# Moving two small bursts of fp32 products in a scan: the reads beside the next block's masked products, the values' part beside the first corner product

## The chip, the cores and the metric

The kernel runs on one core of one Trainium2 chip. The metric is the device time of one execution in microseconds (us); the median of the runs before the change is 2252.5 us.

## The reference, cut to what matters

One inference step of a hybrid backbone with one layer, on 128 context tokens and 256 latent tokens (384 columns together), model width 2048. A large input projection feeds two branches. Branch A is a scan over time with 32 heads of size 64, once forward and once backward:

```
def step(S, inp):
    r_t, w_t, k_t, v_t, a_t, b_t = inp
    sa = einsum('dbhij,dbhj->dbhi', S, a_t)
    S = S * w_t[..., None, :] + sa[..., :, None] * b_t[..., None, :] + v_t[..., :, None] * k_t[..., None, :]
    y = einsum('dbhij,dbhj->dbhi', S, r_t)
    return S, y
y = ys[0] + ys[1]
mu = mean(y); var = mean((y - mu) ** 2)            # per head
y = ((y - mu) * rsqrt(var + GN_EPS)) * lnx_g + lnx_b
y = y + bonus
y_a = (y * silu(g_a)) @ w_out_a
```

Branch B is a short gated convolution. Both are gated, merged and projected again. The step by sa takes something out of the state ("removal") along a_t; S @ r_t is the "read".

## The kernel before, in words

**The projection stream.** Most of TensorE's work is one long stream of projections (`Stream`, L111). A unit of it is three matmuls (L81 to L83, a product in three parts of 128x128 weights by 384 columns). A pair of 128 output columns takes 32 units. The order of TensorE's work is written out by hand: `ds_.go(n)` emits n units, and between them the code emits the scan's small bursts of plain fp32 matmuls, whose generators yield how many units follow (`drive`, L931). An fp32 matmul that is not a transpose is two instructions in the profile, so 24 of them show as x48. The other engines' queues are ordered by a planner from its own costs and from the order in which the code emits, with `high_priority` for the scan.

**A block.** The scan works through 16 blocks of two heads (`for b in range(NB)`, L949), each cut into 6 chunks of 64 tokens a direction, 12 in all (index f). In a chunk the steps are solved together with a 64x64 triangular inverse, made from two 32x32 diagonal inverses and a corner.

- `prep_b` (L664) makes the operands pr and bk on VectorE, waits PB0 = 14 units, and emits the masked products: a burst of pA (L700) for one direction, masks on VectorE (L706) into the tile A, PB1 = 6 units, and the same for the other direction. It then writes the 32x32 diagonal blocks out through DRAM (L710), loads them as U (L716), inverts them on VectorE with 60 dependent operations (L721, L723), transposes them on ScalarE (UT, L727), and brings both back through DRAM into A (L734) and x11 (L735). POOL scales bk in between (L713).
- `prep_c` (L737) transposes the values into sav (pv, L755) and the keys into bt (pb, L764), a unit behind each. Then comes the values' part of the removals: pav (L770), 24 products of A's rows 64 to 127 with the values, four copies on ScalarE into sav (L774), and a clearing of A's used part on POOL (L777). It ends with sums for the bonus and a transpose of the state that is loaded (psi, L786).
- The driver goes on with the stream until the pair gv{b} is done, and then `prep_a` (L608) of the next block with its products; at least WINDOW = 80 units lie between the masked products and the scan.
- `scan` (L790) begins with the first corner product pH (L848 by way of L852), which needs A and x11, copies it into x11 (L854), starts the second chain (po, L810; the sum into sav on VectorE, L811), makes the second corner product pX (L867) and copies it into A (L869). Two chains then run through the chunks in bursts of two matmuls (po, pq, pu). At the end it reads within the chunks: py (L889), 24 products of A's second half with sav, added to the tile ytok on VectorE (L892). The states are transposed and written out (pso, L896).
- `norm` (L903) normalises ytok: VectorE, with one operation on ScalarE (L912) and one on POOL (L917). It is emitted behind the scan.
- `finish` (L920) of a block is emitted in the next one, just ahead of its masked products: three transposes (L924), then scale, bonus and gate (L926 to L928) and a write to ya_d (L929).

**What is shared.** The scan's PSUM results rotate through five banks (`bank`, L590). SP's queue issues nearly all DMAs in order: the weights' (L101, L104), the blocks' and the results'.

Of the kernel before, what the change touches and what calls it, by code (L numbers as in the profile page):

```python
# [12 lines left out]
ALU = mybir.AluOpType  # L13
AX = mybir.AxisListType

P = 128
# [4 lines left out]
NB = 16  # L21
C = 64
NCH = 6
# [33 lines left out]
def hybrid_step(ctx, tc, cst, x_prompt, x_sample, state_f, state_b, c, c_ctx, ada_w, ada_b, norm_g,  # L57
# [3 lines left out]
    V, S, G, TE = nc.vector, nc.scalar, nc.gpsimd, nc.tensor  # L61
# [120 lines left out]
    ds_ = Stream()  # L182
# [218 lines left out]
    r_, k_, v_, ga_ = {}, {}, {}, {}  # L401
# [188 lines left out]
    def bank(nm):  # L590
        return ps1.tile([P, 4, P], F32, tag="A", name=nm, bufs=5)
# [4 lines left out]
    def flat(a):  # L596
        return a.rearrange("p n t -> p (n t)")
# [66 lines left out]
    def prep_b(b, o):  # L664

        r, kk = r_[b], o["kk"]
        o["pr"], o["bk"] = [], []
        for d in range(2):
            ep, em, kd, bn = o["ep"][d], o["em"][d], o["kd"][d], o["bn"][d]
            pr = sp.tile([P, NCH, P], F32, tag=f"pr{d}", name=f"pr_{b}_{d}")  # L670
            bk = sp.tile([P, NCH, P], F32, tag=f"bk{d}", name=f"bk_{b}_{d}")
            V.tensor_tensor(bk[:, :, 0:C], c3(bn[:]), c3(em[:]), ALU.mult)
            V.tensor_tensor(bk[:, :, C:P], c3(kd[:]), c3(em[:]), ALU.mult)
            V.tensor_tensor(pr[:, :, 0:C], c3(kk[:, ::-1] if d else kk[:]), ep[:, :, 0:C], ALU.mult)
            r3 = c3(r[:])
            if d == 0:
                V.tensor_tensor(pr[:, :, C:P], r3, ep[:, :, 1:C + 1], ALU.mult)
            else:
                V.tensor_tensor(pr[:, :, C:P], r3[:, ::-1, :], ep[:, :, C:0:-1], ALU.mult)
            o["pr"].append(pr)  # L680
            o["bk"].append(bk)
        yield PB0

        def blocks(A, d, e):

            es = slice(32 * e, 32 * e + 32)
            return A[es, 0, NCH * d:NCH * d + NCH, :].rearrange("s n (h t) -> s (n h) t", h=2)[:, :, es]

        ui = dp.tile([2, 2, 12, 32, 32], F32, tag="ui", name=f"ui_{b}", bufs=2)
        uo = dp.tile([2, 2, 2, 12, 32, 32], F32, tag="uo", name=f"uo_{b}", bufs=2)  # L690

        A = sp.tile([P, 2, 2 * NCH, P], F32, tag="A", name=f"A_{b}")
        o["A"] = A
        for d in range(2):
            pr, bk = o["pr"][d], o["bk"][d]
            m0 = C_MB if d else C_MF
            pas = {(h, n0): bank(f"pA_{b}_{d}_{h}_{n0}") for n0 in (0, 4) for h in range(2)}
            for n in range(NCH):
                for h in range(2):
                    TE.matmul(pas[h, n // 4 * 4][:, n % 4, :], bk[hss[h], n, :], pr[hss[h], n, :],  # L700
                              start=True, stop=True)
            for n0, w in ((0, 4), (4, 2)):
                mk = cs[:, m0:m0 + P].rearrange("p (w t) -> p w t", t=C).unsqueeze(1).broadcast_to([P, w, 2, C])
                for h in range(2):
                    f0 = NCH * d + n0
                    V.tensor_tensor(A[:, :, f0:f0 + w, hss[h]].rearrange("p w n t -> p n w t"),  # L706
                                    pas[h, n0][:, 0:w, :].rearrange("p n (w t) -> p n w t", t=C), mk, ALU.mult)
            yield PB1
            for e in range(2):
                nc.sync.dma_start(ui[d, e].rearrange("i s t -> s i t"), blocks(A, d, e))  # L710

        for d in range(2):
            G.tensor_tensor(o["bk"][d][:], o["bk"][d][:], o["ep"][d][:, :, C:C + 1].broadcast_to([P, NCH, P]), ALU.mult)  # L713

        U = sp.tile([48, 32, 32], F32, tag="U", name=f"U_{b}")
        nc.sync.dma_start(U[:], ui[:].rearrange("d e i s t -> (d e i) s t"))  # L716
        ut = sp.tile([48, 256], F32, tag="ut", name=f"ut_{b}")
        for s in range(1, 31):
            w = 31 - s
            tv = ut[:, 0:s * w].rearrange("p (a b) -> p a b", b=w)  # L720
            V.tensor_tensor(tv, U[:, 0:s, s:s + 1].broadcast_to([48, s, w]),  # L721
                            U[:, s:s + 1, s + 1:].broadcast_to([48, s, w]), ALU.mult)
            V.tensor_tensor(U[:, 0:s, s + 1:], U[:, 0:s, s + 1:], tv, ALU.add)  # L723
        dg = U[:].rearrange("p a b -> p (a b)")[:, 0:1024:33]
        V.tensor_scalar(dg, dg, 1.0, None, ALU.add)
        UT = sp.tile([48, 32, 32], F32, tag="UT", name=f"UT_{b}")
        S.copy(UT[:], U[:].rearrange("p a b -> p b a"))  # L727
        nc.sync.dma_start(uo[0].rearrange("d e i s t -> (d e i) s t"), U[:])
        nc.sync.dma_start(uo[1].rearrange("d e i s t -> (d e i) s t"), UT[:])
        x11 = sp.tile([64, 24, 32], F32, tag="x11", name=f"x11_{b}")  # L730
        o["x11"] = x11
        for d in range(2):
            for e in range(2):
                nc.sync.dma_start(blocks(A, d, e), uo[0, d, e].rearrange("i s t -> s i t"))  # L734
            nc.sync.dma_start(x11[0:32, 12 * d:12 * d + 12, :], uo[1, d, 0].rearrange("i s t -> s i t"))  # L735

    def prep_c(b, o):  # L737

        r, v, A = r_[b], v_[b], o["A"]
        for d in range(2):  # L740
            for h in range(2):
                nc.sync.dma_start(s_in[d][hss[h], hss[h]], ctx_st[d][0, 0, 2 * b + h])
# [16 lines left out]
        for d in range(2):  # L759

            for n0, n1 in (((0, 4), (4, 5)), ((0, 3), (4, 6)))[d]:
# [2 lines left out]
                    TE.transpose(pb[:, n - n0, :], o["bk"][d][:, n, :], ident)  # L764
                S.copy(bt[:, NCH * d + n0:NCH * d + n1, :], pb[:, 0:n1 - n0, :])
                yield 1
        pvs = [bank(f"pav_{b}_{d}") for d in range(2)]
        for f in range(2 * NCH):
            for h in range(2):
                TE.matmul(flat(pvs[f // NCH][hss[h]])[:, C * (f % NCH):C * (f % NCH) + C], A[C:P, 0, f, hss[h]],  # L770
                          sav[C:P, f, hss[h]], start=True, stop=True)
        for d in range(2):
            for h in range(2):
                S.copy(sav[0:C, NCH * d:NCH * d + NCH, hss[h]],  # L774
                       flat(pvs[d][hss[h]])[:, 0:NCH * C].rearrange("p (n i) -> p n i", i=C))

        G.memset(A[C:P, 0, :, :], 0.0)  # L777
        yield 2
        ks = o["kd"]
        V.tensor_tensor(ks[0][:], ks[0][:], ks[1][:, ::-1], ALU.add)  # L780
        V.scalar_tensor_tensor(ks[0][:], ks[0][:], pcol(RK + b), r[:], ALU.mult, ALU.mult)
# [8 lines left out]
    def scan(b, o):  # L790
# [52 lines left out]
        def corner(nm, lhs, rhs):  # L843
# [5 lines left out]
                              start=True, stop=True)  # L849
            return [flat(pz[32 * j:32 * j + 32])[:, 0:192].rearrange("p (n t) -> p n t", t=32) for j in range(4)]  # L850

        pz = corner("pH", lambda f, h: A[0:32, 0, f, C * h + 32:C * h + C], lambda f, h: x11[0:32, 2 * f + h, :])  # L852
        for j in range(4):
            (S.copy, V.tensor_copy)[j % 2](x11[32:64, j::4, :], pz[j])  # L854
        yield H0
        lat = chain(1)
        next(lat)
# [22 lines left out]
                else:  # L880
                    yield CH0 if len(live) > 1 else CH1

        py = bank(f"py2_{b}")
        for q in range(3):
            for h in range(2):
                for d in range(2):
                    for e in range(2):
                        f = 2 * q + e if d == 0 else NCH + 5 - 2 * q - e
                        TE.matmul(py[hss[e], q, hss[h]], A[:, 1, f, hss[h]], sav[:, f, hss[h]],  # L889
                                  start=d == 0, stop=d == 1)  # L890
        yield 1
        V.tensor_tensor(ytok[:], ytok[:], py[:, 0:3, :], ALU.add)  # L892

        pt = bank(f"pso_{b}")
        for d in range(2):
            TE.transpose(pt[:, d, :], st[0][:, d, :], ident)  # L896
        for d in range(2):
# [2 lines left out]
                S.copy(nst[hss[h], :], pt[hss[h], d, hss[h]])  # L900
            nc.sync.dma_start(ctx_ns[d][0, 0, 2 * b:2 * b + 2].rearrange("h i j -> (h i) j"), nst[:])

    def norm(b, o):  # L903

        ytok = o["ytok"]
        y6 = ytok[:].rearrange("p q (h i) -> p (q h) i", i=C)
        mu = sp.tile([P, 6], F32, tag="mu", name=f"mu_{b}")
        V.tensor_reduce(mu[:], y6, AX.X, ALU.add)
        V.tensor_scalar(mu[:], mu[:], 1.0 / C, None, ALU.mult)
        V.tensor_tensor(y6, y6, mu[:].unsqueeze(2).broadcast_to([P, 6, C]), ALU.subtract)  # L910
        sq = tmp(f"ysq_{b}")
        S.activation(sq[:], flat(ytok[:]), AF.Square)  # L912
        var = sp.tile([P, 6], F32, tag="var", name=f"var_{b}")
        V.tensor_reduce(var[:], sq[:].rearrange("p (q i) -> p q i", i=C), AX.X, ALU.add)
        V.tensor_scalar(var[:], var[:], 1.0 / C, GN_EPS, ALU.mult, ALU.add)  # L915
        rs = sp.tile([P, 6], F32, tag="rs", name=f"rs_{b}")
        G.tensor_tensor(rs[:], var[:], nhalf[:], ALU.pow)  # L917
        V.tensor_tensor(y6, y6, rs[:].unsqueeze(2).broadcast_to([P, 6, C]), ALU.mult)
# [26 lines left out]
    cur = {}  # L945
# [3 lines left out]
    for b in range(NB):  # L949
# [5 lines left out]
        pb_gen = prep_b(b, cur)  # L955
        ds_.go(next(pb_gen))
        if prev is not None:
            finish(b - 1, prev)
        drive(pb_gen)
        n = drive(prep_c(b, cur))  # L960
        nxt = {}
        if b < NB - 1:
            while f"gv{b}" not in ds_.done:
# [10 lines left out]
                prep_k(b + 1, nxt)  # L974

        drive(scan(b, cur), 300, 3 if b < NB - 1 else None, keys)
        norm(b, cur)
        prev, cur = cur, nxt
    ds_.go(12)
    finish(NB - 1, prev)  # L980
    ctx_sc.close()

# [177 lines left out]
```

## Time and profile before

| | |
|---|---|
| median of 3 runs | 2252.5 us (2251.61 to 2254.43) |
| the profiled execution | 2250.97 us, its span 2249.2 us |
| granted TensorE clock of it | 0.996 |
| DVE, ACT, POOL busy | 68%, 47%, 5% of the span |
| chain that ended last | PE 84%, DVE 6%, DMA 6%, ACT 2% |

PE is TensorE's matmuls, PEld its weight loads, DVE VectorE, ACT ScalarE, POOL GpSimd, SP the engine that issues DMAs (SPq, its queue). A row of the timeline has the start (us from the span's start), the length, engine, line, operation, output tile <- input tiles, shapes, how many were merged, and in brackets the engine's idle time ahead of it and what ended that. The numbers ahead of a matmul's shape, as in 64\*64, are the rows and columns of TensorE that it uses. In a row of the windows view each engine has its busy time and count of instructions. Matmuls overlap in the records, so a burst's cost is read from start to start.

### The profile page before, as it was taken

Reading aid. Unit: us, or ns where it says so; the run is one execution under the profiler, and the core shown is the slowest. Engines: PE = TensorE matmul, PEld = TensorE weight load, DVE = VectorE, ACT = ScalarE, POOL = GpSimd, SP = SyncE. Lnnn points to the kernel's source line nnn. Section 1 sums busy time; section 2 is a strip of 40 time slices with the busy share of each in tenths; the row PEclk is TensorE's granted clock in tenths of the full one; section 3 lists DMA queues with packets and bytes.
Section 4 is the critical chain, followed back from the end, with each engine's and each line's share of the span. In section 5 each row is a group of like instructions: output and inputs, shape, how many; then the busy total and the mean of one; then the engine's idle time right before and its main releaser. Section 6 shows DMA issues by size and latency. Waiting matters only on the chain.

```text
span 2249.2 us, 40427 instructions
## 1 busy us (share of the span) xinstructions
PE 2191.4 (97%) x16084; PEld 2071.0 (92%) x16084; DVE 1522.2 (68%) x3096; ACT 1060.7 (47%) x1864; POOL 115.5 (5%) x115
## 2 busy tenths in 40 slices
PE   6999999999999999999999999999999999999998
PEld 3588999999999999999999999999999999889988
DVE  3249567787777778777878787777767774444454
ACT  4245445454545455455545454546455543333233
POOL 2000010101010100000010101010100000000000
PEclk9999999999999999999999999999999999999999
DMA  9963544444444445354434444344445455985633
GB/s 337 346 204 116 146 130 131 111 129 114 111 132 112 120 119 125 111 132 106 126 102 132 111 117 127 110 122 135 121 125 139 147 175 162 312 303 185 220 131 113
DMA packets 429644, 339.96 MB, mean 151 GB/s; under 512 B 84800, under 2 KB 411024, under 8 KB 428560
## 3 DMA queue, kind: packets, MB, share of 16 engines
q1 hardware_dynamic: 427968, 335.62, 51.0%
q8 instruction: 127, 2.08, 0.4%
q10 hardware_dynamic: 432, 1.57, 0.2%
q14 instruction: 61, 0.50, 0.1%
q0 software_dynamic: 1056, 0.19, 0.1%
HBM read 307.37 MB, written 29.36 MB: 150 GB/s over the span
## 4 chain that ended last, share of the span: by engine, by line
PE 84%; DVE 6%; DMA 6%; ACT 2%; issue 1%; SPq 1%; POOLq 0%; POOL 0%; DVEq 0%; ACTq 0%
PE d_rk L81 4%; PE d_rk L83 4%; PE d_rk L82 4%; DMA raw_adah<-in_ada_w_dram 4%; PE d_gv L81 4%; PE d_gv L83 4%; PE d_gv L82 4%; PE d_oa L81 2%; PE pA L700 2%; PE d_oa L83 2%; PE d_oa L82 2%; PE d_mb L81 2%; PE d_bc L81 2%; PE d_gb L81 2%; PE d_bg L81 2%; PE d_mb L83 2%
## 5 line engine op out<-in xcount | busy, mean ns | idle before, releaser
L81 PE MATMUL d_rk<-h_hi,whi_rk 128*128 128x384 f32 x480 | 164.4, 342 | 0.6 <-ACT lst L549 0.6
L721 DVE TENSOR_TENSOR ut<-U 48x30 f32<-48x30 f32 (+14 forms) x480 | 154.5, 322 | 15.3 <-DMA U<-ui 2.5
L723 DVE TENSOR_TENSOR U<-U,ut 48x30 f32<-48x30 f32 (+14 forms) x480 | 154.2, 321 | 11.2
L81 PE MATMUL d_gv<-h_hi,whi_gv 128*128 128x384 f32 x480 | 161.1, 336 | 0.0
L83 PE MATMUL d_gv<-h_hi,wlo_gv 128*128 128x384 f32 x480 | 161.0, 335 | 0.0
L82 PE MATMUL d_gv<-h_lo,whi_gv 128*128 128x384 f32 x480 | 160.9, 335 | 0.0
L83 PE MATMUL d_rk<-h_hi,wlo_rk 128*128 128x384 f32 x480 | 160.6, 335 | 0.0
L82 PE MATMUL d_rk<-h_lo,whi_rk 128*128 128x384 f32 x480 | 160.6, 334 | 0.0
L88 ACT CAST whi_gv<-raw_gv 128x1024 fp32r<-128x1024 f32 (+1 forms) x64 | 64.0, 1000 | 139.7 <-PE d_rk L82 94.0
L89 DVE TENSOR_TENSOR wlo_rk<-raw_rk,whi_rk 128x1024 fp32r<-128x1024 f32 x60 | 72.9, 1218 | 44.6 <-ACT whi_rk L88 40.0
L88 ACT CAST whi_rk<-raw_rk 128x1024 fp32r<-128x1024 f32 x60 | 63.0, 1053 | 79.6 <-PE d_gb L82 16.4
L81 PE MATMUL d_bc<-h_hi,whi_bc 128*128 128x384 f32 x256 | 92.5, 361 | 0.0
L81 PE MATMUL d_gb<-h_hi,whi_gb 128*128 128x384 f32 x256 | 92.5, 361 | 0.0
L81 PE MATMUL d_bg<-h_hi,whi_bg 128*128 128x384 f32 x256 | 92.4, 361 | 0.0
L81 PE MATMUL d_bx<-h_hi,whi_bx 128*128 128x384 f32 x256 | 92.4, 361 | 0.0
L81 PE MATMUL d_ma<-h_hi,whi_ma 128*128 128x384 f32 x256 | 92.0, 359 | 0.0
L81 PEld LDWEIGHTS d_rk<-h_hi,whi_rk 128*128 128x128 f32 x480 | 90.1, 188 | 1.8 <-ACT lst L549 0.9
L917 POOL TENSOR_TENSOR rs<-var,nhalf 128x6 f32<-128x6 f32 x16 | 21.2, 1325 | 1361.8 <-DVE var L915 1361.8
L81 PE MATMUL d_mb<-h_hi,whi_mb 128*128 128x384 f32 x256 | 90.6, 354 | 0.0
L81 PEld LDWEIGHTS d_gv<-h_hi,whi_gv 128*128 128x128 f32 x480 | 90.4, 188 | 0.2
L83 PEld LDWEIGHTS d_gv<-h_hi,wlo_gv 128*128 128x128 f32 x480 | 90.4, 188 | 0.0
L82 PEld LDWEIGHTS d_gv<-h_lo,whi_gv 128*128 128x128 f32 x480 | 90.4, 188 | 0.0
(320 smaller groups left out, 6660.1 us busy)
## 6 DMA issues: line engine op xcount, KB each, us to landing
raw_adah<-in_ada_w_dram SPq DMA_DIRECT2D x64, 512.0 KB, 8.6
raw_rk<-in_w_in_dram SPq DMA_DIRECT2D x60, 512.0 KB, 5.3
raw_gv<-in_w_in_dram SPq DMA_DIRECT2D x60, 512.0 KB, 5.0
raw_ma<-in_w_in_dram SPq DMA_DIRECT2D x16, 1024.0 KB, 5.5
raw_mb<-in_w_in_dram SPq DMA_DIRECT2D x16, 1024.0 KB, 5.4
raw_bc<-in_w_in_dram SPq DMA_DIRECT2D x16, 1024.0 KB, 5.5
raw_bx<-in_w_in_dram SPq DMA_DIRECT2D x16, 1024.0 KB, 5.4
raw_bg<-in_w_in_dram SPq DMA_DIRECT2D x16, 1024.0 KB, 5.5
```

Source lines behind the costliest of these rows:

```text
L81: TE.matmul(out, wh, xh, start=start, stop=False)
L82: TE.matmul(out, wh, xl, start=False, stop=False)
L83: TE.matmul(out, wl, xh, start=False, stop=stop)
L88: S.copy(hi[0:rows], src)
L89: V.tensor_tensor(lo[0:rows], src, hi[0:rows].bitcast(F32), ALU.subtract)
L700: TE.matmul(pas[h, n // 4 * 4][:, n % 4, :], bk[hss[h], n, :], pr[hss[h], n, :], start=True, stop=True)
L721: V.tensor_tensor(tv, U[:, 0:s, s:s + 1].broadcast_to([48, s, w]), U[:, s:s + 1, s + 1:].broadcast_to([48, s, w]), ALU.mult)
L723: V.tensor_tensor(U[:, 0:s, s + 1:], U[:, 0:s, s + 1:], tv, ALU.add)
L917: G.tensor_tensor(rs[:], var[:], nhalf[:], ALU.pow)
```

## The change

The change moves three things and renames nothing that is computed. The same matmuls are issued.

1. **Values' part.** The burst pav leaves `prep_c` and stands at the start of `scan`, straight ahead of the first corner product, with no unit of the stream between them. Its four copies to sav and the clearing of A come behind the copies of the corner. The `yield 2` behind pav goes.
2. **Reads.** The burst py2 leaves the end of `scan`, with its `yield 1`, and becomes a function `reads`, which is called in the next block between the 14 units and the first masked product. Its sum into ytok is now the first operation of `norm`.
3. **Norm and finish.** `norm` of block b-1 is emitted behind `prep_b` of block b, its VectorE operations held behind the last masked product's (`issue_after`). `finish` of block b-1 is emitted behind `prep_c` of block b instead of ahead of the masked products. For the last block reads, norm and finish follow the loop, with 13 units ahead of finish instead of 12.

```
@@ prep_b: the last mask is kept
-                    V.tensor_tensor(A[:, :, f0:f0 + w, hss[h]].rearrange("p w n t -> p n w t"),
-                                    pas[h, n0][:, 0:w, :].rearrange("p n (w t) -> p n w t", t=C), mk, ALU.mult)
+                    o["masked"] = V.tensor_tensor(
+                        A[:, :, f0:f0 + w, hss[h]].rearrange("p w n t -> p n w t"),
+                        pas[h, n0][:, 0:w, :].rearrange("p n (w t) -> p n w t", t=C), mk, ALU.mult).ins
@@ prep_c
-        pvs = [bank(f"pav_{b}_{d}") for d in range(2)]
-        for f in range(2 * NCH):
-            for h in range(2):
-                TE.matmul(flat(pvs[f // NCH][hss[h]])[:, C * (f % NCH):C * (f % NCH) + C], A[C:P, 0, f, hss[h]],
-                          sav[C:P, f, hss[h]], start=True, stop=True)
-        for d in range(2):
-            for h in range(2):
-                S.copy(sav[0:C, NCH * d:NCH * d + NCH, hss[h]],
-                       flat(pvs[d][hss[h]])[:, 0:NCH * C].rearrange("p (n i) -> p n i", i=C))
-
-        G.memset(A[C:P, 0, :, :], 0.0)
-        yield 2
@@ scan, its start
+        pvs = [bank(f"pav_{b}_{d}") for d in range(2)]
+        for f in range(2 * NCH):
+            for h in range(2):
+                TE.matmul(flat(pvs[f // NCH][hss[h]])[:, C * (f % NCH):C * (f % NCH) + C], A[C:P, 0, f, hss[h]],
+                          sav[C:P, f, hss[h]], start=True, stop=True)
         pz = corner("pH", lambda f, h: A[0:32, 0, f, C * h + 32:C * h + C], lambda f, h: x11[0:32, 2 * f + h, :])
         for j in range(4):
             (S.copy, V.tensor_copy)[j % 2](x11[32:64, j::4, :], pz[j])
+        for d in range(2):
+            for h in range(2):
+                S.copy(sav[0:C, NCH * d:NCH * d + NCH, hss[h]],
+                       flat(pvs[d][hss[h]])[:, 0:NCH * C].rearrange("p (n i) -> p n i", i=C))
+
+        G.memset(A[C:P, 0, :, :], 0.0)
         yield H0
@@ scan, its end: py2 and the sum leave, the states' transposes stay
-        yield 1
-        V.tensor_tensor(ytok[:], ytok[:], py[:, 0:3, :], ALU.add)
...
+    def reads(b, o):
+
+        A, sav, ytok = o["A"], o["sav"], o["ytok"]
         py = bank(f"py2_{b}")
...
+        o["py"] = py
 
     def norm(b, o):
 
         ytok = o["ytok"]
+        V.tensor_tensor(ytok[:], ytok[:], o["py"][:, 0:3, :], ALU.add)
@@ the loop over the blocks
         pb_gen = prep_b(b, cur)
         ds_.go(next(pb_gen))
         if prev is not None:
+            reads(b - 1, prev)
+        drive(pb_gen)
+        if prev is not None:
+            with tc.issue_after(cur["masked"]):
+                norm(b - 1, prev)
+        n = drive(prep_c(b, cur))
+        if prev is not None:
             finish(b - 1, prev)
-        drive(pb_gen)
-        n = drive(prep_c(b, cur))
...
         drive(scan(b, cur), 300, 3 if b < NB - 1 else None, keys)
-        norm(b, cur)
         prev, cur = cur, nxt
-    ds_.go(12)
+    reads(NB - 1, prev)
+    norm(NB - 1, prev)
+    ds_.go(13)
     finish(NB - 1, prev)
```

More of the change, by code (lines that the diff above doesn't have):

```diff
@@ L737, in prep_c @@
     def prep_c(b, o):
-        r, v, A = r_[b], v_[b], o["A"]
+        r, v = r_[b], v_[b]
         for d in range(2):
@@ L881, in scan @@
                     yield CH0 if len(live) > 1 else CH1
+        pt = bank(f"pso_{b}")
+        for d in range(2):
+            TE.transpose(pt[:, d, :], st[0][:, d, :], ident)
+        for d in range(2):
+            nst = sp.tile([P, C], F32, tag="ns", name=f"ns_{b}_{d}")
+            for h in range(2):
+                S.copy(nst[hss[h], :], pt[hss[h], d, hss[h]])
+            nc.sync.dma_start(ctx_ns[d][0, 0, 2 * b:2 * b + 2].rearrange("h i j -> (h i) j"), nst[:])
+    def reads(b, o):
+        A, sav, ytok = o["A"], o["sav"], o["ytok"]
         py = bank(f"py2_{b}")
@@ L890, in scan @@
                                   start=d == 0, stop=d == 1)
-        yield 1
[L892 to L897, printed above, removed]
-            nst = sp.tile([P, C], F32, tag="ns", name=f"ns_{b}_{d}")
-            for h in range(2):
-                S.copy(nst[hss[h], :], pt[hss[h], d, hss[h]])
-            nc.sync.dma_start(ctx_ns[d][0, 0, 2 * b:2 * b + 2].rearrange("h i j -> (h i) j"), nst[:])
+        o["py"] = py
     def norm(b, o):
         ytok = o["ytok"]
+        V.tensor_tensor(ytok[:], ytok[:], o["py"][:, 0:3, :], ALU.add)
         y6 = ytok[:].rearrange("p q (h i) -> p (q h) i", i=C)
```

## The prediction

> **What bounds the kernel now.** I read the page first, then who made TensorE wait, then TensorE's timeline around the bursts that the change joins, then the path on which the first corner product depends.
>
> ```profile
> span 2249.2 us, 40427 instructions
> ...
> PE 2191.4 (97%) x16084; PEld 2071.0 (92%) x16084; DVE 1522.2 (68%) x3096; ACT 1060.7 (47%) x1864; POOL 115.5 (5%) x115
> ```
>
> TensorE is busy for 97% of the span. Its longest wait lies in the prologue, which the change leaves alone:
>
> ```profile
> PE pada L289 <- DMA raw_adah<-in_ada_w_dram: 21.6, 14, 10.0
> ```
>
> So inside the 16 blocks the time is what TensorE needs to issue a fixed list of matmuls, plus what it loses where one kind of burst follows another. The change adds and removes no matmul and no unit of the projection stream. It can gain only at the edges of bursts, and lose only where TensorE, which keeps the written order, comes to wait. An edge in block 6 (timeline of TensorE: start, length, what):
>
> ```profile
> 854.71 0.33 PE L82 MATMUL d_rk<-h_lo,whi_rk 128*128 128x384 f32 x1
> 854.88 0.34 PE L83 MATMUL d_rk<-h_hi,wlo_rk 128*128 128x384 f32 x1
> 855.15 1.61 PE L770 MATMUL pav<-sav,A 64*64 64x64 f32 x48
> 856.69 0.45 PE L81 MATMUL d_rk<-h_hi,whi_rk 128*128 128x384 f32 x1
> 856.98 0.34 PE L82 MATMUL d_rk<-h_lo,whi_rk 128*128 128x384 f32 x1
> ```
>
> Projection matmuls start 0.17 us apart (854.71 to 854.88), so a unit of three takes 0.52. From the last one ahead of the burst to the second one behind it are 2.10 us, of which 0.35 are two projection steps: the burst costs 1.75. Its pace inside is read from the counts of two nested windows over tile pav alone:
>
> ```profile
> 855.40:855.90 0.50, 0.50 (x25) 0.50 (x21) 0.00 (x0) 1.00 1.16 164
> 855.40:856.40 1.00, 1.00 (x42) 1.00 (x38) 0.29 (x1) 1.00 1.18 192
> ```
>
> The second half microsecond adds 17 matmul instructions, 29 ns each, so 48 are 1.40 us of work. The other 0.35 us are edges. About 0.20 lie behind the burst: its last matmul starts near 856.54 (855.15 + 1.61, less some 0.22 for the last one), the next projection matmul comes 0.15 later where 0.06 is the step of a pair, the one after that 0.29 later where 0.17 is usual. The remaining 0.15 lie ahead: 855.15 is 0.27 behind 854.88, 0.10 too late, and the rest is a slow first pair.
>
> **Part 1: the joins.** The reads (tile py, L889) stand alone at the end of each block's scan:
>
> ```profile
> 934.86 0.34 PE L83 MATMUL d_gb<-h_hi,wlo_gb 128*128 128x384 f32 x1
> 935.12 1.62 PE L889 MATMUL py<-sav,A 128*64 128x64 f32 x48
> 936.67 0.44 PE L81 MATMUL d_bc<-h_hi,whi_bc 128*128 128x384 f32 x1
> 936.95 0.34 PE L82 MATMUL d_bc<-h_lo,whi_bc 128*128 128x384 f32 x1
> ```
>
> They cost 2.09 - 0.35 = 1.74, as pav does, with the same 0.35 of edges. The change puts pav straight ahead of the first corner product pH in 16 blocks, and the reads of block b-1 straight ahead of the masked products pA of block b 15 times (block 15's reads stay alone): 31 joins. What a join saves hangs on the boundary that remains, since the partners use TensorE in different shapes, 128\*64 then 64\*128 and 64\*64 then 32\*32. No such boundary is in the trace of before. Its ends: it costs nothing, and a join saves 0.35 (10.9 us in all); or it costs a full exit and entry, and a join saves nothing. The nearest row is a 64\*128 burst entered from something other than a projection, the transposes of finish:
>
> ```profile
> 839.89 0.34 PE L83 MATMUL d_bx<-h_hi,wlo_bx 128*128 128x384 f32 x1
> 840.07 0.49 PE L924 MATMUL py<-cs,ytok 128*128 128x128 f32 x3
> 840.49 1.61 PE L700 MATMUL pA<-pr,bk 64*128 64x128 f32 x24
> 842.03 0.44 PE L81 MATMUL d_bx<-h_hi,whi_bx 128*128 128x384 f32 x1
> 842.31 0.33 PE L82 MATMUL d_bx<-h_lo,whi_bx 128*128 128x384 f32 x1
> ```
>
> The transposes step by 0.11 ((0.49 - 0.27) / 2, with 0.27 for one), the last starts at 840.29, and pA follows 0.20 later, 0.09 too late. That is the lateness with which pav was entered from a projection (0.10): entering a shape costs the same, whatever stood ahead. So I take the remaining boundary at one entry, 0.15. A join then turns two entries and two exits (0.70) into two entries and one exit (0.50) and saves 0.20: 31 x 0.20 = **6.2 us**.
>
> The Trainium skill speaks against more: "TensorEngine Tiling (Array Packing)", section Key Properties, says that changing the tiling mode, not merely the tile, drains TensorE. By that rule both joins keep a drain between their shapes and the sum is the 6.2; without it the sum would be 10.9. The 0.09 above agrees with it, but no run yet shows two tiled shapes side by side.
>
> The three transposes of finish leave the pA burst and become a burst of their own, 3 x 0.11 there as here; they were entered at 840.07 with no lateness (0.18 against 0.17), so I give them no edge. The end of that burst may cost up to 0.11 (what the second matmul behind pav lost), 1.7 us over 15 blocks; I take 0.
>
> **Part 2: the path to the corner.** pH needs the inverse blocks, which VectorE makes in U (L721, L723) and DMAs carry to x11. In block 6 the last mask, the load of U, and two stages, from masks to U and through U (columns PE, PEld, DVE, ACT, POOL busy):
>
> ```profile
> 846.56 1.95 DVE L706 TENSOR_TENSOR A<-pA,cs 128x512 f32<-128x512 f32 x4 [0.65 <-PE pA L700]
> ```
>
> ```profile
> 848.50:856.80 8.30, 8.30 (x94) 7.78 (x92) 4.97 (x9) 7.06 (x14) 0.14 (x1) 1.00 0.67 147
> 856.80:887.10 30.30, 30.30 (x176) 30.27 (x177) 28.96 (x81) 11.72 (x17) 1.38 (x1) 1.00 0.39 112
> ```
>
> ```profile
> 895.10 1.08 SPq L735 DMA_DIRECT2D x<-uo  x1
> ```
>
> ```profile
> DMA to landing us min/median/max: 2.9/4.1/5.4
> ```
>
> ```profile
> 898.44 0.34 PE L634 MATMUL pn<-lo_sq,bones_r 128*128 128x384 f32 x1
> 898.71 0.38 PE L848 MATMUL pH<-x,A 32*32 32x32 f32 x22
> ```
>
> The last x11 transfer, issued at 895.10, lands 2.9 us later (5.4 would be past pH's own start), at 898.0. pH starts at 898.71 unhindered: cover 0.7 us. The tightest is block 5:
>
> ```profile
> 788.49 0.98 SPq L735 DMA_DIRECT2D x<-uo  x1
> ```
>
> ```profile
> DMA to landing us min/median/max: 3.7/4.7/5.8
> ```
>
> ```profile
> 792.53 0.56 PE L848 MATMUL pH<-x,A 32*32 32x32 f32 x42
> ```
>
> There 788.49 + 3.7 is 792.19, 0.34 ahead of pH. Worked the same way, ten blocks have 0.3 to 1.2, four (4, 8, 12, 15) have over 2.3, and blocks 0 and 1 have 9 and more. This cover changes in three ways.
>
> TensorE arrives later by 0.6. The loop ahead of the corner runs until gv{b} is done, at a fixed place in the stream; counted from the yields, pH now stands behind 82 units instead of 81 (+0.52), behind finish (+0.33), and still behind pav, which moves with it and saves 0.20. Pav itself needs nothing of x11.
>
> VectorE gets norm between the last mask and U. Its ops in the trace of before, undisturbed (first and last):
>
> ```profile
> 832.67 0.55 DVE L892 TENSOR_TENSOR ytok<-ytok,py 128x384 f32<-128x384 f32 x1
> ...
> 837.46 0.56 DVE L918 TENSOR_TENSOR ytok<-ytok,rs 128x384 f32<-128x384 f32 x1 [1.50 <-POOL rs L917]
> ```
>
> That is 5.35 us from end to end. VectorE is idle for 8.30 - 4.97 = 3.3 us in that stage and norm's own ops there need some 3.1, so it about fits, with the weight splits waiting a little. A split that waits holds the next weight load on SP's queue, and U's load is queued behind that; I take 0.3 of delay, with 0 and one op of 0.56 as ends.
>
> Finish now comes during U, where VectorE is 96% busy, so its two ops lengthen U:
>
> ```profile
> 841.30 0.56 DVE L927 TENSOR_TENSOR ya<-ya,bon 128x384 f32<-128x384 f32 x1 [2.15 <-ACT ya L926]
> 841.89 0.56 DVE L928 TENSOR_TENSOR ya<-ya,ga 128x384 f32<-128x384 f32 x1
> 842.37 1.94 DVE L706 TENSOR_TENSOR A<-pA,cs 128x512 f32<-128x512 f32 x4
> ```
>
> Starts of such ops are 0.48 apart (841.89 to 842.37), so 0.95 (0 if they run in a gap of U, 1.2 with both waits). Delay 1.25 against cover 0.7 + 0.6: about even. In the ten tight blocks I book 0.12 each, **1.2 us lost**. Two more queues are passed. On SP the write of ya_d moves from ahead of ui to behind U's load and waits there for finish, with a weight load behind it; no projection waits for its weights now, so I take 0, at worst finish's 0.95 once a block. On POOL the clearing of A moves out of U's stage, where it was all that POOL did (1.38 us), to the scan's start: 0.
>
> **Part 3: the rest of the scan's start.** Pav's four copies to sav and the clearing of A move there. ACT had room around pH:
>
> ```profile
> 899.37 0.31 ACT L854 COPY x<-pH 32x192 f32<-32x192 f32 x1 [1.39 <-PE pH L848]
> 900.10 0.31 ACT L854 COPY x<-pH 32x192 f32<-32x192 f32 x1 [0.42 <-DVE x L854]
> 901.93 1.05 ACT L88 CAST whi_gb<-raw_gb 128x1024 fp32r<-128x1024 f32 x1 [1.52 <-PE d_bg L82]
> ```
>
> ```profile
> L774 ACT COPY sav<-pav 64x384 f32<-64x384 f32 x64 | 30.4, 476 | 3.1 <-PE pav L770 2.3
> ```
>
> Idle 1.39 + 0.42 + 1.52 = 3.3 us against 4 x 0.476 = 1.9, so I take 0; if one copy falls ahead of a copy that the next product needs, 0.48 in 16 blocks, 7.6 us. Queued behind the copies on ACT are the scan's ytok copies, behind the sum on VectorE (L811) the next corner's copies. The reads' bank stays taken until norm, so pA's second set has four banks instead of five: the masks of the first set end at 844.31 (842.37 + 1.94) and those of the second begin at 846.56, so 0. Norm's last op must precede the transposes of finish, 14 units and 12 transposes behind pA, about 8.6 us; norm starts some 2 us into that and takes 5.35, so 1 us of cover, 0.
>
> **The sum.** -6.2 + 1.2 = -5.0 us. The profiled execution took 2250.97 us, its span 2249.2; the median of the runs shown is 2252.5, 1.5 above. Applied to the median: **2247.5 us**. A measurement of this kernel can tell about 0.2%, 4.5 us, from no change: faster is below 2248.0, slower above 2257.0. The forecast lies just below the first bound.
>
> **The rivals.** (a) No drain between shapes: a join saves 0.35, with the 1.2 lost 2242.8. For it: pav reads partitions 64 to 127 and pH 0 to 31, so these two share no operand. Against it: the 0.09 ahead of pA. (b) A boundary between two shapes costs exit and entry: nothing saved, 2253.7. For it: no row of this kind exists. (c) The copies of pav stand in the way of the second corner's: 2247.5 + 7.6 = 2255.1. For it: the in-order queues; against it, ACT's idle 3.3 us. (d) Slower: norm doesn't fit ahead of U. If half of its 3.1 us of VectorE ops, and its wait for POOL (1.50), run inside U together with finish, the path is 1.55 + 1.0 + 0.95 = 3.5 us later against 1.3 of cover: 2.2 us of wait for x11 in the ten tight blocks and 0.6 in the four wide ones, so 24.4 - 6.2 = 18.2 more, 2270.7; with half of that wait in the tight blocks alone 11 - 6.2 = 4.8 more, 2257.3. It eats the gain from 0.6 us of wait a tight block (6.2 / 10), and passes the upper bound from 1.1. For it: VectorE's 96% in U; against it: norm is ready long before U lands.
>
> **How the numbers follow.** Forecast 0.46 (its own range 2244.5 to 2248.0, the booked wait between 0 and 0.2 a block), (a) 0.07: faster 0.53. (b) 0.10, (c) or small waits 0.18: within 0.28. (d) 0.19: slower. The range for 8 in 10 runs from (a)'s 2242.8, rounded to 2242.5, to a little into (d), 2259.0; it leaves out (d)'s far part.
>
> **What the changed profile would show.** Right: the timeline has pA some 0.15 behind the last read and pH as closely behind the last pav, and two edges of 0.20 fewer a block; the masks-to-U stage holds norm, U's stage is about 1 us longer, and TensorE's waits for x11 stay near 1 us in all. Wrong: joined bursts as long as the two apart (b), a line of TensorE waiting for DMA x or for ytok with several us in all (d), or pX or pq waiting for ACT (c).

## The result and the profile after

| | before | after |
|---|---|---|
| median of 4 runs | 2252.53 us (2251.61 to 2254.43) | 2280.77 us (2276.8 to 2283.57) |
| profiled execution, its span | 2250.97, 2249.2 us | 2281.94, 2280.0 us |

The ratio is 1.0122, with an interval of 1.011 to 1.0134: the change costs 28 us, where a gain of 5 was forecast. Lines of the changed kernel after L706 have other numbers (vr L753, pv L756, reads L902, finish L928). Its page and chain:

```profile
span 2280.0 us, 40462 instructions
...
PE 2198.7 (96%) x16084; PEld 2077.3 (91%) x16084; DVE 1514.4 (66%) x3096; ACT 1055.6 (46%) x1864; POOL 116.6 (5%) x115
...
PE 62%; DVE 23%; DMA 7%; issue 4%; ACT 4%; SPq 1%; POOL 0%; DVEq 0%; POOLq 0%; ACTq 0%
```

No engine has markedly more to do than before (PE 2191.4 to 2198.7, DVE 1522.2 to 1514.4). But VectorE's share of the chain that ended last went from 6% to 23%: TensorE now stops for other engines. Its waits in after (us in all, times, longest) show where:

```profile
PE pl L83 <- DVE lwl L89: 10.6, 14, 1.9
PE pv L756 <- ACT vr L753: 7.7, 15, 3.4
PE pl L81 <- ACT lwh L88: 7.1, 7, 1.7
```

In before the second didn't exist, and the other two were 1.9 and 1.3 us, once each. The tile pl holds the products of `prep_a` with the decay weights. These weights come in two pairs; each is cast by ScalarE into lwh, and VectorE writes what the cast leaves over into lwl. The tile vr is ScalarE's reversed copy of the values, for the second burst of pv.

**The joins are there.** After's timeline around the reads and the values' part of block 6:

```profile
846.49 0.34 PE L83 MATMUL d_bx<-h_hi,wlo_bx 128*128 128x384 f32 x1
846.76 1.62 PE L902 MATMUL py<-sav,A 128*64 128x64 f32 x48
848.30 1.61 PE L700 MATMUL pA<-pr,bk 64*128 64x128 f32 x24
...
850.12 0.34 PE L82 MATMUL d_bx<-h_lo,whi_bx 128*128 128x384 f32 x1
...
909.63 0.34 PE L634 MATMUL pn<-lo_sq,bones_r 128*128 128x384 f32 x1
909.90 1.61 PE L845 MATMUL pav<-sav,A 64*64 64x64 f32 x48
911.45 0.62 PE L837 MATMUL pH<-x,A 32*32 32x32 f32 x48
...
912.27 0.34 PE L82 MATMUL d_bg<-h_lo,whi_bg 128*128 128x384 f32 x1
```

The first burst costs 850.12 - 846.49 - 0.35 = 3.28 us, the second 2.29. Read in the same way from every block, the medians are 3.289 and 2.294. Apart they were 1.751 + 1.744 and 1.752 + 0.756 in before. So a join saves 0.206 and 0.214 us, and all of them 15 x 0.206 + 16 x 0.214 = 6.5 us.

**Where the time went.** Summed from start to start of neighbouring matmuls, after against before:

| step of TensorE | us |
|---|---|
| to pv and within it | +12.6 |
| to, within and from pl | +22.4 |
| from projection to projection | +4.3 |
| the joins | -6.5 |

That is 32.8; the two profiled executions differ by 31.0, and the other steps together are some 1.8 shorter.

**The vr queue.** In before, the copy vr was made long ahead of its products (the tile's starts, first and last of two blocks; the first weight load of its products starts at 850.8 in the first of them, the last at 955.9 in the second):

```profile
L752 ACT COPY vr<-v x2: 501/501/501, 841.2 to 945.9; 128x384 f32<-128x384 f32 x2
```

In after, ScalarE has been idle for 4.85 us, and vr still stands behind norm's square (L916), which waits for VectorE behind the last mask:

```profile
856.93 1.06 ACT L88 CAST whi_rk<-raw_rk 128x1024 fp32r<-128x1024 f32 x1 [4.85 <-PE d_bx L82]
858.19 0.53 ACT L916 ACTIVATE ysq<-ytok 128x384 f32<-128x384 f32 x1 [0.21 <-DVE ytok L914]
858.62 0.49 ACT L753 COPY vr<-v 128x384 f32<-128x384 f32 x1
859.14 1.94 ACT L758 COPY sav<-pv 64x384 f32<-64x384 f32 x4
```

The 12.6 us aren't spread evenly. In 13 of the blocks pv takes 0.44 us more than before, in block 1 it takes 1.7 more, and in block 15 it takes 5.2 more. There TensorE first waits for the masked products' tile A (2.6 us in before), then for vr, and runs at half clock from 1827.3 on:

```profile
1827.16 0.78 PE L756 MATMUL pv<-cs,v 128*128 128x128 f32 x3 [3.70 <-DVE A L706]
...
1832.29 0.90 PE L756 MATMUL pv<-cs,vr 128*128 128x128 f32 x3 [3.40 <-ACT vr L753]
```

**The decay queue.** The stages of block 6 that the prediction used, from the last mask to U and through U, in after (columns PE, PEld, DVE, ACT, POOL, PEclk):

```profile
856.31:865.41 9.10, 8.88 (x59) 8.32 (x58) 7.29 (x17) 8.15 (x17) 1.44 (x2) 1.00 0.64 139
865.41:898.64 33.23, 33.23 (x193) 33.23 (x193) 31.99 (x84) 11.06 (x15) 0.00 (x0) 1.00 0.39 108
```

They were 8.30 and 30.30 us: U ends 3.7 us later. What follows on ScalarE in after is one row of in-order work, and what TensorE makes of it stands in the second fence:

```profile
898.64 2.09 ACT L728 COPY UT<-U 48x1024 f32<-48x1024 f32 x1 [2.90 <-DVE U L724]
900.64 0.47 ACT L412 COPY zs<-d_gv 128x384 f32<-128x384 f32 x1
901.01 0.57 ACT L413 ACTIVATE v<-d_gv,cm 128x384 f32<-128x384 f32 x1
901.48 1.04 ACT L88 CAST whi_bg<-raw_bg 128x1024 fp32r<-128x1024 f32 x1
902.42 0.53 ACT L615 ACTIVATE sq<-kk 128x384 f32<-128x384 f32 x1
902.98 0.51 ACT L604 CAST sqh<-sq 128x384 fp32r<-128x384 f32 x1
903.40 0.40 ACT L88 CAST lwh<-lraw 96x256 fp32r<-96x256 f32 x1
```

```profile
898.18 0.34 PE L81 MATMUL pl<-l_hi,lwh 96*128 96x384 f32 x1
...
903.85 0.45 PE L81 MATMUL pl<-l_hi,lwh 96*128 96x384 f32 x1 [1.28 <-ACT lwh L88]
...
905.01 0.44 PE L83 MATMUL pl<-l_hi,lwl 96*128 96x384 f32 x1 [0.54 <-DVE lwl L89]
...
906.19 0.52 PE L82 MATMUL d_bg<-h_lo,whi_bg 128*128 128x384 f32 x1
906.51 0.52 PE L83 MATMUL d_bg<-h_hi,wlo_bg 128*128 128x384 f32 x1
```

ScalarE has been waiting for U; behind UT stand six operations, the last of them the cast of the second pair. The tile lwh holds both pairs in turn, but that isn't what held the cast: the last product of the first pair with lwh starts at 899.95, and the cast, with no idle time of ScalarE ahead of it, at 903.40. In before, UT stood 3.7 us ahead of the first product of pl, and the cast was done in time:

```profile
887.15 2.14 ACT L727 COPY UT<-U 48x1024 f32<-48x1024 f32 x1 [0.42 <-DVE U L723]
...
893.00 0.41 ACT L88 CAST lwh<-lraw 96x256 fp32r<-96x256 f32 x1 [0.25 <-PE pl L82]
```

```profile
890.86 0.34 PE L81 MATMUL pl<-l_hi,lwh 96*128 96x384 f32 x1
```

In after it stands 0.46 behind (898.18 to 898.64). Of these 4.2 us, counted from the last mask, 3.7 are U's, and 0.5 TensorE's, which comes to pl earlier now that pav no longer stands ahead of it. The last two rows of the timeline are 0.32 us apart instead of 0.17: TensorE runs at half clock there, as the PEclk of two windows over after says (0.50 in the second).

```profile
902.30:905.71 3.41, 1.59 (x8) 1.00 (x7) 2.66 (x7) 3.38 (x8) 0.00 (x0) 1.00 0.23 51
905.71:909.12 3.41, 3.41 (x13) 3.41 (x12) 1.22 (x1) 1.03 (x2) 0.00 (x0) 0.50 0.63 96
```

By the trace's clock there are 23.9 us of half clock between 250 and 2200 us in after, against 3.4 in before. Four stretches of 3.4 stand behind stops at pl; the other 10.2 stand at block 15's pv, where before has its 3.4. Half of the 20.5 more, some 10 us, is a part of the 12.6, 22.4 and 4.3 above. The waits for lwl and lwh (10.6 + 7.1 - 3.2 = 14.5) are most of the 22.4.

### The profile page after: what moved, and what is told of

Read it like the earlier page. It is cut to its first block, busy times and chain, and to the rows that moved or that the text cites. A ratio compares the mean times of both kernels' runs of the same rounds, so it can differ in the third digit from the quotient of the medians.

```text
span 2280.0 us, 40462 instructions
## 1 busy us (share of the span) xinstructions
PE 2198.7 (96%) x16084; PEld 2077.3 (91%) x16084; DVE 1514.4 (66%) x3096; ACT 1055.6 (46%) x1864; POOL 116.6 (5%) x115
## 4 chain that ended last, share of the span: by engine, by line
PE 62%; DVE 23%; DMA 7%; issue 4%; ACT 4%; SPq 1%; POOL 0%; DVEq 0%; POOLq 0%; ACTq 0%
DVE ut L722 4%; DVE U L724 4%; DMA raw_adah<-in_ada_w_dram 3%; DVE wlo_gv L89 2%; PE d_oa L81 2%; PE d_oa L83 2%; PE d_oa L82 2%; PE pA L700 2%; PE d_mb L81 2%; PE d_mb L83 2%; PE d_mb L82 2%; PE d_bg L81 2%; PE d_gb L81 1%; PE d_bg L83 1%; PE d_bg L82 1%
## 5 line engine op out<-in xcount | busy, mean ns | idle before, releaser
L706 DVE TENSOR_TENSOR A<-pA,cs 128x256 f32<-128x256 f32 (+1 forms) x128 | 62.3, 548 | 57.6 <-PE pA L700 57.5
L81 PE MATMUL d_ob<-ybh,whi_ob 128*128 128x384 f32 x256 | 89.5, 350 | 1.7 <-DVE smb L516 1.0
```

The source lines that it names most:

```text
L81: TE.matmul(out, wh, xh, start=start, stop=False)
L706: o["masked"] = V.tensor_tensor(A[:, :, f0:f0 + w, hss[h]].rearrange("p w n t -> p n w t"), pas[h, n0][:, 0:w, :].rearrange("p n (w t) -> ...
```

## The experiments

The theories: that the loss is these two queues, each a cost of its own (vr behind norm's square; the cast behind a late U); that one of them only shows because of the other; that something else in the moved norm or finish costs. Letters in a quoted expectation are its own. Ratios are to before, with the 95% interval.

**Each half alone.** *Values only*: before, with pav and its copies moved to the scan. *Reads only*: after, with pav back in `prep_c`.

> Only the values' part moves (pav and its copies to the first corner product); reads, norm and finish stay as before. Theory A (the joins save as forecast; the loss comes from the late path through U and from ACT's queue order, both owed to reads, norm and finish): 16 joins at 0.21 us, so 2249.1 us, no new wait of TensorE at pv or pl. Rival B (the values' part itself loses time: its copies crowd the scan's start, and without pav TensorE comes 1.75 us earlier to pl): above 2255.

> Only reads, norm and finish move; pav stays in prep_c. Theory A: the wait at pv for vr stays whole (some 12 us), the waits at pl stay in part, since pav gives U 1.75 us more per block: 5 to 10 us of them; 15 joins save 3.1. In all 2267 to 2272 us. Rival B: close to the time before, 2249 to 2253.

Measured: values only 2260.36 us, 1.0045 [1.0032, 1.0057]; reads only 2258.76, 1.0039 [1.0026, 1.0051]. Both miss their theories: the halves cost 9 and 7 us, and both at once 28. Values only lies where its rival put it, by the rival's second ground: TensorE is early at pl. Reads only lies between its two ranges. TensorE's waits, values only and then reads only:

```profile
PE pl L83 <- DVE lwl L89: 7.2, 10, 1.9
...
PE pl L81 <- ACT lwh L88: 1.8, 2, 1.5
PE pH L836 <- DMA x<-uo: 1.4, 1, 1.4
```

```profile
PE pv L756 <- ACT vr L753: 7.6, 15, 3.3
...
PE pl L83 <- DVE lwl L89: 2.7, 3, 1.9
PE pl L81 <- ACT lwh L88: 1.4, 1, 1.4
```

The vr queue belongs to the reads' half. The decay queue belongs to both: without pav ahead of it TensorE is early, with norm and finish ahead U is late, and the slack takes up most of either one (decay waits of 9.0 and 4.1 us against 3.2 in before), but not of both (17.7).

**The copy vr ahead of norm.**

```
+        cur["vr"] = tmp(f"vr_{b}")
+        S.copy(cur["vr"][:], v_[b][:, ::-1])
         if prev is not None:
             with tc.issue_after(cur["masked"]):
                 norm(b - 1, prev)
```

> The changed kernel with the reversed copy of the values (vr) written ahead of norm, so that it stands ahead of norm's square on ACT's queue. Theory A, with the waits in series on one path: the wait at pv goes, but TensorE then comes 0.8 us earlier to pl, and its waits there grow by most of that: 2274 to 2281 us. Rival C (the waits are independent and add up): 12 us less, 2268.

2270.16 us, 1.0088 [1.0074, 1.0101]: 10.6 less than after by the medians, some 8 by the ratios. The row for vr is gone, the decay rows stay. So the two queues add up:

```profile
PE pl L83 <- DVE lwl L89: 9.2, 14, 1.9
PE pl L81 <- ACT lwh L88: 8.8, 7, 1.6
```

**Fewer units ahead of the masked products.** PB0 = 8 instead of 14 brings the masks, and so U, 3.1 us earlier against the fixed place of pl: in after, in after with early vr, in before, and in values only; and 11 with early vr.

> The changed kernel with 8 instead of 14 units ahead of the masked products, so masks and U start 3.1 us earlier beside the same later work; VectorE has the operands ready 9 us ahead. Theory A: the waits at pl (22 us) and the half-clock stretches that go with them (4 us) vanish, the wait at pv stays: about 2255 us. Rival D (pl waits for an ACT or VectorE that is simply too busy there, not for U): little changes, over 2272.

> The changed kernel with both: vr written ahead of norm and 8 units instead of 14 ahead of the masked products. Theory A as amended (two waits that add up: pv for vr behind norm's square on ACT, pl for casts behind U): both gone, what is left are the 31 joins: 2252.5 - 6.4, about 2246 us, at most 4 more for VectorE's operands in the first block. Rival E (something else of the change costs as well, such as the copies in the scan's start): above 2252.

> As e5_pb0_8_vr with 11 units: 1.56 us more for U than in e3_vr_early instead of 3.1. Theory A: lateness at pl in e3 is some 1.5 us a block, so most of it goes: 2246 to 2254 us. Rival E: above 2258.

> The kernel before with 8 units instead of 14 ahead of the masked products, nothing else. Theory A: before, TensorE waits for neither pv nor pl, so more time for U gains nothing: within 0.2% of before (2250 to 2256, up to 4 lost in the first block). Rival F (shorter PB0 is a gain of its own, and e4 and e5 gain from that): 2246 or less.

> Only the values' part moved, as in e1_values_only, with 8 units instead of 14. Theory A: e1's waits at pl come from TensorE reaching pl 1.75 us earlier without pav ahead of it; 3.1 us more for U take them away, and the 16 joins are left: 2252 - 3.4 = 2248 us, up to 4 more in the first block. Rival B (the copies crowd the scan's start): stays near e1's 2260.

| | us | ratio |
|---|---|---|
| after, 8 | 2270.5 | 1.0086 [1.0072, 1.0099] |
| after, 8, early vr | 2245.67 | 0.9975 [0.9966, 0.9985] |
| after, 11, early vr | 2261.53 | 1.0047 [1.0034, 1.006] |
| before, 8 | 2279.24 | 1.0123 [1.011, 1.0136] |
| values only, 8 | 2274.06 | 1.0101 [1.0088, 1.0114] |

After with 8 misses its 2255: the decay rows are down to two each, but the wait for vr has grown to 22.2 us. With both mended the kernel is a little faster than before, as expected. With 11 it misses its 2246 to 2254: half of the decay waits remain (7.3 + 2.3). Before and values only with 8 miss: their finish stands straight behind those units, and waits for norm. The row of before with 8:

```profile
PE py L924 <- DVE ytok L918: 22.1, 15, 2.8
```

So it is the moved norm and finish that allow the shorter lead.

**Finish out of U.** After with early vr, and finish straight ahead of the scan.

> e3_vr_early with finish moved from ahead of the wait for gv to straight ahead of the scan, so that its two VectorE operations no longer stand within U. Theory A: U ends some 1 us earlier in each block and the waits at pl shrink by about as much in 14 blocks: 2255 to 2262 us against e3's 2270. Rival H (finish has no share in U's lateness): 2268 or more.

2256.3 us, 1.0024 [1.0014, 1.0035], as expected: 13.9 less than with early vr alone. With finish's two VectorE operations out of U, the decay rows go from 9.2 and 8.8 to 6.7 and 4.7, which is 6.6 us; and the 13.7 us of half clock between 250 and 2200 us with early vr alone are gone, half of which is 6.8.

**The casts ahead of U, first try.** Both pairs cast at the start of `prep_a`, their raw weights in two of the eight shared scratch tiles.

> e3_vr_early with both weight pairs of prep_a loaded and cast at its start, with a buffer each (the raw weights in buffers that are there), so that the second pair's casts need not stand behind the copy UT on ACT. Theory A (TensorE waits at pl because those casts are queued behind UT): the waits at pl go, and with U as late as before x11 is the next to be late, up to 1 us a block: 2250 to 2260 us. Rival G (U is late by itself, and TensorE loses the same at pH instead): 2266 or more.

> e1_values_only with the same early casts. Theory A: its waits at pl (9 us) and the half-clock stretch go, the 16 joins are left: 2247 to 2251 us. Rival G: near e1's 2260.

> e5_pb0_8_vr with the same early casts. Theory A: e5 has almost no waits at pl left (5 us, in the first blocks), so 0 to 4 us less: 2242 to 2246 us. Rival (the early casts gain or lose by themselves): outside that.

2394.05, 2399.09 and 2373.84 us (1.0635 [1.062, 1.0649], 1.0652 [1.0638, 1.0667], 1.0546 [1.0531, 1.056]). These don't test the queue: the raw weights lost their early load. SP's queue in the first of the three:

```profile
940.21 0.33 SPq L734 DMA_DIRECT2D uo<-UT  x1
940.58 0.42 SPq L623 DMA_DIRECT2D lraw<-in_w_dram  x1
```

The load is issued behind the result of U, and TensorE waits for lwh for 96.1 us in all, 27 times. With early vr alone, the pair that is cast at 900.7 had been loaded ahead of 810.

**The casts ahead of U, with tiles of their own.** Both pairs are loaded and cast ahead of the masked products, in separate tiles (room comes from letting the inverse's scratch and the states written out share other tiles): in after with early vr, in values only, in the best version (8, early vr), and in before.

```
+        nxt = {}
+        if b < NB - 1:
+            nxt["lw"] = [pair(b + 1, m) for m in (0, 2)]
         pb_gen = prep_b(b, cur)
```

> The changed kernel with the early copy vr (2270.2), and both pairs of decay weights cast ahead of the masked products, now with two raw tiles of their own, so that their loads stay early; the inverse's scratch tile and the tile of the states written out share other tiles for the room. Theory (the casts stand in ScalarE's queue behind the transpose of U): the rows of TensorE waiting for lwh and lwl go to under 2 us, the stretches of half clock with them, and the time to 2246 to 2252. Rival (U itself is late, and the wait moves on): TensorE, no longer stopped at the decay products, comes earlier to the first corner product and waits there for x11, 0.5 to 1.5 us a block; 2254 to 2264.

> Before with only the values' part moved (2260.4), and the same early casts with tiles of their own. Theory: waits for lwl and lwh (7.2 + 1.8 us) gone, 2247 to 2252, the joins of the values showing. Rival: the wait moves to the first corner product (1.4 us for x11 becomes 5 or more): 2253 to 2260.

> The changed kernel with 8 units and the early vr (2245.7), and both pairs cast early with tiles of their own. Waits for lwl and lwh there were 2.9 + 1.9 us in all: theory 2241 to 2246. Rival (the casts now stand ahead of other work that TensorE waits for): 2247 to 2252.

> Before, unmoved, with both pairs of decay weights cast early in tiles of their own: a control for the best version. Theory (before lost only 1.9 + 1.3 us to lwl and lwh, so its decay products have little to gain): 2247 to 2252. Rival (the early casts free ScalarE and VectorE for something else and are themselves the gain of the best version): 2243 to 2246.

| | us | ratio |
|---|---|---|
| after, early vr | 2256.41 | 1.0023 [1.0014, 1.0031] |
| values only | 2253.26 | 1.001 [1.0, 1.0019] |
| after, 8, early vr | 2240.98 | 0.9956 [0.9944, 0.9967] |
| before | 2247.52 | 0.9985 [0.9976, 0.9994] |

In the first, no wait for lwh or lwl is left among the rows over 1 us, so the cast's place in ScalarE's queue is the cause of those waits. (The separate tiles also end the reuse of lwh; the rows of after above show that the queue came last.) But theory and rival both hold: the time is 13.8 less, not the theory's 18 to 24, because TensorE now comes early to the first corner product and waits there:

```profile
PE pH L841 <- DMA x<-uo: 5.4, 7, 1.1
```

The stops at pl had hidden how late U is. A price of the early casts comes on top: in block 0 TensorE waits 5.1 us for pr, VectorE's operand of the first masked product, where it was 1.0. Values only likewise goes to 4.6 us in 6 waits for x11. With 8 units U is early enough for both. The last two rows of the table differ by 6.5 us (the intervals leave some 3 either way). That this is just what the joins were worked out to save is in part luck, since the wait for pr differs too: it is 5.1 us in the last row and 8.3 with 8 units:

```profile
PE pA L705 <- DVE pr L682: 8.3, 1, 8.3
```

Before with early casts is 3.6 faster. Its decay waits of 1.9 + 1.3 are gone, but it pays 4.1 more for pr; what makes up the difference wasn't taken apart.

**Finish out of U in the best versions** (8 and early vr; the same with early casts).

> The changed kernel with 8 units ahead of the masked products and the early vr (2245.7), and finish moved to straight ahead of the scan, out of U. Theory (with 8 units no wait is left to take away, so only small ones can shrink): 2244 to 2247. Rival (finish's two operations in U still cost): 2240 to 2243.

> The best version so far (8 units, early vr, both pairs early, 2241.0) with finish moved to straight ahead of the scan. Theory (no wait in the blocks is left for it to shorten): 2239.5 to 2242.5. Rival (finish's operations in U still cost): under 2239.

2244.47 us, 0.9971 [0.9961, 0.9981], and **2238.93 us**, 0.9948 [0.9936, 0.9961]. The second lies just under the 2239 below which its rival began. But the intervals overlap with those of the versions they start from, so the 1.2 and 2.0 us aren't shown. The last has the lowest median of all, 12.2 us below before.

## Why the prediction was wrong, point by point

**Part 1 held.** 6.2 us forecast, 6.5 measured. Of the 0.35 of a burst's edges a join keeps some 0.14, about what was taken for one entry. Rivals (a), no drain, and (b), full edges, are out: they would have shown 0.35 and 0 where 0.206 and 0.214 stand. The rule of the Trainium skill, "TensorEngine Tiling (Array Packing)", section Key Properties, agrees with the trace, since the boundary between two tiled shapes isn't free. The three transposes of finish, given no edge, cost 0.337 as a burst of their own, against 2.065 - 1.744 = 0.321 ahead of pA.

**The step that failed is part 2, "1.2 us lost".** It followed the late U to one consumer, x11 and pH. Two others were left out.

- The cast of the second decay pair stands behind UT on ScalarE, and pl comes ahead of pH. The sentence "no projection waits for its weights now, so I take 0" looked at SP's queue alone. What it missed measured 22.4 us at pl, with the half clock behind it. The prediction counted TensorE's way to pH, where pav still stands ahead; on the way to pl it doesn't, and its 1.75 us of cover are gone.
- "VectorE gets norm between the last mask and U" is true, and in that order ScalarE's square came to stand ahead of vr. Part 3 went through ScalarE's queue at the scan's start and not here. The steps at pv measured 12.6 us more, 1.1 of them a longer wait for A in block 15.

**A size in the same part.** Norm "about fits", 0.3 us of delay: 0.8 measured in block 6. Finish's 0.95 in U: U became 2.9 longer, VectorE's work in it 3.0 (28.96 to 31.99). Counted by tile in block 6, U has finish's two operations more (0.95), one weight split more (8 instead of 7, 1.23 each), which norm displaced from the stage ahead, the gate's product, since U now runs until gv is done, and one copy of the state less. By their lengths these come to 2.4 of the 3.0; the rest isn't accounted for. In blocks 5 and 7 it is two splits more (8 instead of 6).

**Rival (d)** had the sign and the cause, norm and finish making U late, and would have given up to 2270.7. It put the loss at pH. In after TensorE hardly waits there, as forecast, but by luck: it had already stopped at pl. With the casts early the wait for x11 appears, 5.4 us, as (d) has it.

**Part 3 held.** With the two queues mended, no wait at the copies of pav or for a PSUM bank shows among the rows over 1 us, and rival (c) has no row. Finish waits for norm once, 1.4 us, in after.

## What to carry to other kernels

When an operation becomes later, list all that stands behind it in its engine's in-order queue, and for each the place where TensorE needs it; the consumer in the data flow is only one of them, and the first one reached sets the price. A gap of 3 us on an engine is not room for 3 us of new work if other work is due in it: that work goes somewhere, here into the chain. And when a wait is removed, look for the next one behind it, which the first has hidden.

## What the runs showed of the hardware

A stop of under 2 us can cost more than itself. Inside the blocks of after, half clock comes in stretches of 3.4 us and one of 10.2, three times that, so the windows here are 3.41 us long. In after's two windows above, TensorE is busy for 1.59 us of 3.41, and the next 3.41 us run at half clock, though it is busy in all of them. The Trainium skill, "TensorE: Matmul & The Clock Gate", section Part 1, The HAM clock gate, has the clock fall after an idle window of some 3.4 us; here a window a little less than half busy was enough, and the measurement decides.

But TensorE's busy time alone doesn't say when the clock falls. A window of after and one of values only with 8 units, each with the window behind it:

```profile
1117.40:1120.81 3.41, 1.85 (x9) 1.45 (x9) 2.80 (x5) 3.32 (x7) 0.00 (x0) 1.00 0.25 44
1120.81:1124.22 3.41, 3.41 (x12) 3.41 (x12) 0.63 (x1) 0.58 (x1) 0.00 (x0) 0.50 0.71 141
```

```profile
406.38:409.79 3.41, 1.50 (x9) 1.18 (x7) 1.79 (x4) 0.21 (x1) 1.33 (x1) 1.00 0.45 126
409.79:413.20 3.41, 3.33 (x35) 3.07 (x36) 2.04 (x4) 1.66 (x4) 1.09 (x1) 1.00 0.73 196
```

The first, with 1.85 us of work, is followed by half clock; the second, with 1.50, isn't. In after with early vr and early casts, the clock even fell behind a window that was 2.67 us busy, most of it with the joined pav and pH, and held one wait of 0.74 us for x11:

```profile
898.90:902.31 3.41, 2.67 (x100) 2.20 (x99) 1.86 (x4) 2.92 (x7) 1.37 (x1) 1.00 0.68 124
902.31:905.72 3.41, 3.41 (x12) 3.41 (x13) 0.71 (x2) 0.62 (x2) 0.00 (x0) 0.50 0.82 277
```

What decides stays open. Perhaps bursts that use a small part of TensorE count for less; no run tried that by itself.
